# S5 layers of a float32 decoder trunk: order of the stages written by a small list scheduler, float32 in-projections, products moved from GpSimd to VectorE

## Chip, cores and metric

One Trainium2 chip (trn2), one core of it. The metric is device time in microseconds (us) of one execution of the whole program, median of several runs. Engines: TensorE (PE in the profile; PEld is its weight load), VectorE (DVE), ScalarE (ACT), GpSimd (POOL) and SyncE (SP, which here only issues DMAs).

## What is computed

A decoder trunk of four layers on a sequence of T = 512 positions with D = 1024 channels, everything in float32. The layers cycle S5, HGRN2, windowed attention, S5; so layers 0 and 3 are S5. Each layer is `h = h + RMSNorm(branch(RMSNorm(h)))`. The S5 branch, cut to what matters:

```
proj = h @ w_in                       # 1024 x 2048; u = first half, z = second half
xr, xi = einsum(u, bbar_re), einsum(u, bbar_im)   # 64 groups of 16 channels, 64 complex states
s = associative_scan(a, x)            # s[t] = a * s[t-1] + x[t], complex, along the sequence
y = gelu(einsum(c_re, s_re) - einsum(c_im, s_im) + d * u)
y = y * sigmoid(y @ w_glu + b_glu)
out = (y * silu(z)) @ w_out
```

where `a` and `bbar` come from per-group parameters (exp, sin, cos of them).

## The kernel before

**Dense products.** A float32 product of 128 rows of weights with 512 (or 256) columns of activations is made as three products in the float32r type: each operand is split in a high and a low part, and high x high, high x low and low x high are summed (`ws`, `as_`; L146, L160). The weights arrive as raw float32 pieces of 128 x 1024 (`w_load`, tile `wraw`), and `w_conv` splits each: ScalarE copies the high part (`whi`, L112), VectorE subtracts for the low part (`wlo`, L113). The normalised activations are split in the same way by `norm_xt` (`xh` by ScalarE, L210; `xl` by VectorE, L211).

**An S5 layer** (`layer_s5`) works in 16 column blocks of 128 of `w_in`: blocks 0 to 7 give u, 8 to 15 give z. `first_blocks` makes blocks 0 to 3 in two halves of 256 positions each. `s5_tables` computes the small tables of powers of `a` and of rotations from the parameters (`lam`); the sequence is cut in 64 chunks of 8 positions, so that the scan runs over chunks. Then, for each of eight blocks b of 8 groups:

- `s5_block_tables`: loads the block's B and C (`prm`), makes `q`, `vt` (B times powers of a), `w` (C times powers of a), and the taps inside a chunk: `kps`, `kt`, `ktp`, `ksb`, and eight DMAs into `toep`. `vt` is transposed by TensorE (`tps`) into `v`.
- `s5_rot` (once for two blocks): the rotation tables `rot`, copied by DMA into `rotf`.
- `s5_u`: copies the projection to `ut`, writes it to DRAM (`ub`) and reads it back rearranged (`u`).
- `s5_core`: `xps` = v x u on TensorE, swapped halves `xsw` on ScalarE, rotation, real scan and rotation back on VectorE (`xa`, `r`, `rsw`, `spre`), `yps` = u x toep + spre x w on TensorE, gelu into `ysb`, transposes `ytp` into `y`.

Half of the large VectorE products have a partner on GpSimd (`t2`, `t2w`, `rt`, `q12b`, `dmx`, and the subtraction of `w` in odd blocks). After the last block `y` is split into `yh`, `yl` and multiplied with `w_glu` and then `w_out`, as three products each.

**What sets the order.** The text is traced by the Tile framework, which reorders the instructions of each engine by its own cost model and inserts the semaphores. `behind` adds edges that hold some instructions back (`issue_after`). SP issues the weight DMAs, `toep` and `rotf`; ScalarE's queue issues `lam`, `prm`, `dm`, `ub` and `u`. Names in the rows: `pj` is the accumulator of `ws`, `ops` that of the output projection, `t` stands for `t2`, `ap` is the table of powers.

Of the kernel before, what the change touches and what calls it, by code (L numbers as in the profile page):

```python
# [48 lines left out]

class Trunk:  # L50
# [30 lines left out]
    def w_load(self, i):  # L81
        if i >= len(self.wseq) or i in self.wraw or i in self.wcv:
            return
        name, j, c = self.wseq[i]
        shape, pieces = self.w_form(name)
        self.wraw[i] = []
        for v in range(pieces):
            raw = self.wpool.tile(shape, F32, tag="wraw", name="wraw", bufs=3)
            self.nc.sync.dma_start(out=raw, in_=self.a[name][j, c, v])
            self.wraw[i].append(raw)  # L90

    def w_conv(self, i):
        if i >= len(self.wseq) or i in self.wcv:
            return
# [7 lines left out]
        for raw in raws:  # L102
# [72 lines left out]
    def norm_stats(self, L, tbs, h):  # L175

        nc = self.nc
        if tbs[0] == 0:
            self.x = (
                self.act.tile([P, KB, T], F32R, tag="xh", name="xh"),  # L180
                self.act.tile([P, KB, T], F32R, tag="xl", name="xl"),
            )
            self.xs = self.act.tile([P, 4, D], F32, tag="z", name="xs")
# [9 lines left out]
    def norm_xt(self, L, tbs):  # L193
# [7 lines left out]
        for k2 in range(KB // per):  # L201
# [5 lines left out]
            for kk in range(per):  # L207
# [3 lines left out]
                nc.vector.scalar_tensor_tensor(out=xl[:, k, c], in0=ps[:, kk, :], scalar=g, in1=xh[:, k, c].bitcast(F32), op0=ALU.mult, op1=ALU.subtract)  # L211
# [123 lines left out]
    def s5_tables(self, j):  # L335
# [5 lines left out]
        nc.scalar.dma_start(out=lam, in_=a["s5_lam"][j])  # L341
        lr, li, dt = lam[:, 0, :], lam[:, 1, :], lam[:, 2, :]
        nc.scalar.activation(out=dt, in_=dt, func=AF.Exp)
        th = s.tile([P, N], F32, tag="th", name="th", bufs=1)
# [13 lines left out]
        nc.vector.tensor_tensor(out=ap[:, 1, :, 1], in0=mag, in1=sn[:, 0:G], op=ALU.mult)  # L358
        ar, ai = ap[:, 0, :, 1], ap[:, 1, :, 1]
# [64 lines left out]
    def s5_rot(self, pr):  # L424

        nc, s = self.nc, self.scr
        t = self.s5t
        gs = slice(8 * pr, 8 * pr + 8)
        rs = [P, 8, 8, 8]
        rot = s.tile([P, 2, 512], F32, tag="rot", name="rot", bufs=1)  # L430
        rt = self.tab.tile([P, 2, 512], F32, tag="t2", name="rt", bufs=1)
        ro = rot.rearrange("p k (g a b) -> p k g a b", g=8, a=8)
        rr = rt.rearrange("p k (g a b) -> p k g a b", g=8, a=8)
        ea, eb = t["ea"], t["eb"]

        def A(k):
            return bc(ea[:, k, gs, :].unsqueeze(3), rs)

        def Bb(k):
            return bc(eb[:, k, gs, :].unsqueeze(2), rs)  # L440

        nc.vector.tensor_tensor(out=ro[:, 0], in0=A(0), in1=Bb(0), op=ALU.mult)
        nc.gpsimd.tensor_tensor(out=rr[:, 0], in0=A(1), in1=Bb(1), op=ALU.mult)
        nc.vector.tensor_tensor(out=ro[:, 1], in0=A(1), in1=Bb(0), op=ALU.mult)
        nc.gpsimd.tensor_tensor(out=rr[:, 1], in0=A(0), in1=Bb(1), op=ALU.mult)
        nc.vector.tensor_tensor(out=rot[:, 0], in0=rot[:, 0], in1=rt[:, 0], op=ALU.subtract)
        nc.vector.tensor_tensor(out=rot[:, 1], in0=rot[:, 1], in1=rt[:, 1], op=ALU.add)
        out = []
        for i in range(2):
            f = s.tile([P, 2, 512], F32, tag=f"rot{i}", name="rotf", bufs=1)  # L450
# [3 lines left out]
            out.append(f)  # L454
        return out

    def s5_open(self, L):

        self.tabcm = self.tc.tile_pool(name="tab", bufs=1, side="right", reuse_waits="tile")
        self.tab = self.tabcm.__enter__()  # L460
        self.s5_tables(L // 3)

    def s5_block_tables(self, j, b):
        nc, a, s = self.nc, self.a, self.scr
        t = self.s5t
# [12 lines left out]
        s2 = B[:, 3]
        shp = [P, 8, 8, 16]

        vt = self.tab.tile(shp, F32, tag="vt", name="vt", bufs=1)
        t2 = self.tab.tile(shp, F32, tag="t2", name="t2", bufs=1)
        nc.vector.tensor_tensor(out=vt, in0=bc(t["ap"][:, 0, gs, 0:8].unsqueeze(3), shp), in1=bc(q[:, 0].unsqueeze(2), shp), op=ALU.mult)  # L483
# [3 lines left out]
        v = s.tile([P, 8, 128], F32, tag="v", name="v", bufs=2)  # L487
        vtf = vt.rearrange("p g j h -> p g (j h)")
        kps = self.psum.tile([P, 2, 128], F32, tag="ca", name="kps", bufs=2)
        for g in range(8):  # L490
            c = 32 * (g % 4)
            nc.tensor.matmul(kps[c:c + 32, g // 4, :], lhsT=c1[:, g, :], rhs=vtf[:, g, :], start=True, stop=True)
        kt = self.tab.tile([P, 2, 128], F32, tag="q12b", name="kt", bufs=1)
        nc.scalar.activation(out=kt, in_=kps, func=AF.Copy)
        ktp = self.psum.tile([P, 2, 4, 32], F32, tag="ca", name="ktp", bufs=2)
        for i in range(2):
            nc.tensor.transpose(ktp[:, i].rearrange("p g h -> p (g h)"), kt[:, i, :], self.ident)
        dmx = self.tab.tile([P, 8, 16], F32, tag="dmx", name="dmx", bufs=1)
        nc.gpsimd.tensor_tensor(out=dmx, in0=bc(t["dm"][:, gs].unsqueeze(2), [P, 8, 16]), in1=bc(self.cst[:, CO_EYE16:CO_EYE16 + 16].unsqueeze(1), [P, 8, 16]), op=ALU.mult)
        ksb = self.tab.tile([P, 2, 4, 16], F32, tag="ksb", name="ksb", bufs=2)  # L500
        nc.vector.tensor_tensor(out=ksb, in0=ktp[:, :, :, 0:16], in1=dmx.rearrange("p (a g) h -> p a g h", a=2), op=ALU.add)
        toep = self.tp[b % 2]
# [707 lines left out]
```

## Time and profile before

| | |
|---|---|
| median of 3 runs | 1126.23 us (1124.25 to 1127.56) |
| the profiled execution's own time | 1127.56 us |
| its span, first to last instruction | 1125.8 us |
| PE busy | 1039.3 us (92%) |
| DVE busy | 783.4 us (70%) |
| ACT busy | 516.8 us (46%) |
| POOL busy | 233.2 us (21%) |
| granted TensorE clock, mean | 0.968 of 2.4 GHz |

The profile shows one execution. Matmuls are pipelined, and their ends are modelled: an instruction's duration is longer than the distance to the next one, so that a stretch in which PE is "busy" throughout need not be one in which it is at its peak. What one product costs is read from the distance of two starts. In the timeline, "x8" stands for eight like instructions in a row, and the time beside it runs from the first one's start to the last one's end.

### The profile page before, as it was taken

What the parts mean: (1) busy time and instruction counts of PE and PEld (TensorE: products, weight loads), DVE (VectorE), ACT (ScalarE), POOL (GpSimd) and SP (SyncE); (2) the same over time, 40 slices, a digit from 0 to 9 for tenths busy, and PEclk for the clock granted to TensorE, in tenths of its full rate; (3) what the DMA queues carried; (4) which work ended last, traced back from release to release, by engine and by line L of the source; (5) the groups of instructions that cost most, each with busy time, mean ns of one, the idle gap of its engine ahead of it and who ended that gap; (6) DMA issues with size and microseconds to landing.
All of it is one profiled execution on the core that took longest, in us unless ns stands there. A gap on an engine that the chain in (4) does not pass through costs nothing.

```text
span 1125.8 us, 16828 instructions
## 1 busy us (share of the span) xinstructions
PE 1039.3 (92%) x6384; PEld 863.8 (77%) x6384; DVE 783.4 (70%) x1442; ACT 516.8 (46%) x939; POOL 233.2 (21%) x218
## 2 busy tenths in 40 slices
PE   5987898999999999999999989999998888778997
PEld 5866676878899898989888966666688676667885
DVE  6979998675566475656656455566569799995752
ACT  5444444754332324142344344888545254446540
POOL 2165553210200000000001121100011546550200
PEclk9989989999999999999999999999999899998999
DMA  7455425333130212222123443112134644434221
GB/s 244 136 143 141 102 86 128 131 120 114 53 111 22 94 39 83 69 75 76 36 79 102 108 116 100 38 53 80 57 128 126 168 107 139 115 91 140 95 91 56
DMA packets 60320, 112.32 MB, mean 100 GB/s; under 512 B 23632, under 2 KB 33488, under 8 KB 59856
## 3 DMA queue, kind: packets, MB, share of 16 engines
q1 hardware_dynamic: 34272, 87.58, 25.5%
q10 hardware_dynamic: 25968, 23.68, 7.2%
q8 instruction: 50, 0.82, 0.3%
q14 instruction: 30, 0.25, 0.1%
HBM read 87.11 MB, written 8.39 MB: 85 GB/s over the span
## 4 chain that ended last, share of the span: by engine, by line
PE 59%; DVE 23%; issue 6%; DMA 4%; ACT 4%; POOL 3%; ACTq 1%; DVEq 0%; SPq 0%; POOLq 0%
PE pj L146 22%; PE ops L160 14%; PE zps L160 4%; DVE wlo L113 4%; PE vps L160 4%; PE sps L711 2%; PE scps L909 2%; DVE vt L483 2%; PE aops L945 2%; DVE xsw L545 2%; DMA rsw<-rraw 1%; PE ptp L940 1%; DVE vt L485 1%; DMA rotf<-rot 1%; ACT whi L112 1%
## 5 line engine op out<-in xcount | busy, mean ns | idle before, releaser
L146 PE MATMUL pj<-xh,whi 128*128 128x512 f32 (+1 forms) x656 | 238.9, 367 | 0.9 <-ACT whi L112 0.9
L146 PE MATMUL pj<-xh,wlo 128*128 128x512 f32 (+1 forms) x656 | 239.5, 366 | 0.1
L146 PE MATMUL pj<-xl,whi 128*128 128x512 f32 (+1 forms) x656 | 237.9, 364 | 1.3 <-DVE xl L211 1.3
L113 DVE TENSOR_TENSOR wlo<-wraw,whi 128x1024 fp32r<-128x1024 f32 x132 | 172.4, 1311 | 74.5 <-ACT whi L112 67.6
L112 ACT ACTIVATE whi<-wraw 128x1024 fp32r<-128x1024 f32 x132 | 138.6, 1056 | 75.8 <-PE pj L146 31.8
L146 PEld LDWEIGHTS pj<-xh,wlo 128*128 128x128 f32 x656 | 129.0, 197 | 20.6 <-issue 6.1
L146 PEld LDWEIGHTS pj<-xh,whi 128*128 128x128 f32 x656 | 128.9, 198 | 20.5 <-issue 4.8
L146 PEld LDWEIGHTS pj<-xl,whi 128*128 128x128 f32 x656 | 129.0, 197 | 18.2 <-issue 2.7
L160 PE MATMUL ops<-whi,gh 128*128 128x512 f32 x256 | 101.8, 398 | 0.3 <-ACT gh L642 0.3
L160 PE MATMUL ops<-whi,gl 128*128 128x512 f32 x256 | 100.7, 394 | 0.0
L160 PE MATMUL ops<-wlo,gh 128*128 128x512 f32 x256 | 100.3, 392 | 0.0
L160 PEld LDWEIGHTS ops<-whi,gh 128*128 128x128 f32 x256 | 48.2, 188 | 11.3 <-ACT gh L642 1.1
L160 PEld LDWEIGHTS ops<-whi,gl 128*128 128x128 f32 x256 | 48.0, 188 | 11.2 <-DVE gl L643 0.9
L160 PEld LDWEIGHTS ops<-wlo,gh 128*128 128x128 f32 x256 | 48.2, 188 | 10.8 <-issue 1.1
L484 POOL TENSOR_TENSOR t<-ap,q 128x1024 f32<-128x1024 f32 x16 | 40.3, 2519 | 74.6 <-DVE q L475 37.5
L170 POOL TENSOR_SCALAR rs_m<-po_st 128x1 f32<-128x1 f32 x16 | 3.1, 191 | 252.5 <-DVE po_st L256 252.5
L146 PE MATMUL pj<-yh,whi 128*128 128x512 f32 x128 | 49.3, 399 | 4.2 <-ACT yh L621 4.2
L170 POOL TENSOR_SCALAR rs_m<-hss 128x4 f32<-128x4 f32 x8 | 1.6, 194 | 247.9 <-DVE hss L769 247.9
L210 ACT ACTIVATE xh<-xtp,gpre 128x128 fp32r<-128x128 f32 (+1 forms) x96 | 36.2, 400 | 32.8 <-DVE xl L211 20.9
L146 PE MATMUL pj<-yl,whi 128*128 128x512 f32 x128 | 50.1, 393 | 0.0
L146 PE MATMUL pj<-yh,wlo 128*128 128x512 f32 x128 | 50.1, 392 | 0.0
L252 DVE TENSOR_TENSOR yg<-ops,gpost 128x512 f32<-128x512 f32 x32 | 22.0, 689 | 40.0 <-ACT junk L250 39.6
(266 smaller groups left out, 2293.9 us busy)
## 6 DMA issues: line engine op xcount, KB each, us to landing
wraw<-in_s_in SPq DMA_DIRECT2D x32, 512.0 KB, 4.2
wraw<-in_hg_in SPq DMA_DIRECT2D x32, 512.0 KB, 3.5
wraw<-in_at_in SPq DMA_DIRECT2D x20, 512.0 KB, 4.2
rotf<-rot SPq DMA_DIRECT2D x32, 256.0 KB, 4.4
wraw<-in_s_glu SPq DMA_DIRECT2D x16, 512.0 KB, 3.7
wraw<-in_s_out SPq DMA_DIRECT2D x16, 512.0 KB, 3.5
prm<-in_s_bc ACTq DMA_DIRECT2D x16, 256.0 KB, 2.7
ub<-ut ACTq DMA_DIRECT2D x16, 256.0 KB, 3.2
```

Source lines behind the costliest of these rows:

```text
L112: nc.scalar.activation(out=hi, in_=raw, func=AF.Copy)
L113: nc.vector.tensor_tensor(out=lo, in0=raw, in1=hi.bitcast(F32), op=ALU.subtract)
L146: self.nc.tensor.matmul(ps, lhsT=l[k // 4][:, k % 4, c], rhs=r[:, k, n0:n1], start=k == 0 and n == 0, stop=k == KB - 1 and n == 2)
L160: self.nc.tensor.matmul(ps, lhsT=l[:, k, c], rhs=r[k // per][:, k % per, :], start=k == 0 and n == 0, stop=k == KB - 1 and n == 2)
L210: nc.scalar.activation(out=xh[:, k, c], in_=ps[:, kk, :], func=AF.Copy, scale=g)
L252: nc.vector.tensor_tensor(out=yg[:, tb, f], in0=ps, in1=gp[:, f], op=ALU.mult)
L483: nc.vector.tensor_tensor(out=vt, in0=bc(t["ap"][:, 0, gs, 0:8].unsqueeze(3), shp), in1=bc(q[:, 0].unsqueeze(2), shp), op=ALU.mult)
L484: nc.gpsimd.tensor_tensor(out=t2, in0=bc(t["ap"][:, 1, gs, 0:8].unsqueeze(3), shp), in1=bc(q[:, 1].unsqueeze(2), shp), op=ALU.mult)
L545: nc.vector.tensor_tensor(out=xsw, in0=xsw, in1=sin, op=ALU.mult)
L711: nc.tensor.matmul(ps[:, c, :], lhsT=k[:, c * 128:c * 128 + 128], rhs=q4[:, c, :, 1, :], start=True, stop=True)
L909: nc.tensor.matmul(ps[:, bb, lo:256], lhsT=self.q[r, 4 * p + 2 * b2 + bb, qs], rhs=self.k[r, p, ks], start=True, stop=True)
L945: nc.tensor.matmul(ops[64 * i:64 * i + 64].rearrange("p b q -> p (b q)"), lhsT=self.v[:, n - 1 + f, kv * 64:kv * 64 + 64], rhs=pts[i][:, f ...
```

## The change

1. S5's four stages of a block become generators (`s5_v`, `s5_taps`, `s5_w`, `s5_rot`, `s5_u`, `s5_core`), the tables and the 16 in-projections (`s5_rest`) two more. Each yields, ahead of a group of instructions, an engine, a planned duration and the marks that it needs. `Flow.run` takes at each turn the group with the earliest planned start (ties by rank) and lets its generator emit it. The emission runs within `tc.manual_schedule` for PE, DVE, ACT and SP, so that the text's order is the order of these four engines.
2. The in-projections of S5 are made with plain float32 operands, one product in place of three: no split of `w_in` (16 chunks, each 2 pieces, over both layers) and no `xl`. The raw pieces land straight in the tags `whi` and `wlo`, four of each.
3. All products that GpSimd made in the S5 stages are made by VectorE.
4. All DMAs of the S5 stages are issued by SP (`lam`, `prm`, `dm`, `ub`, `u` were ScalarE's).
5. `xps` is made in two column halves of 64 (16 products in place of 8).
6. The order of work within the taps: `v` ahead of `ktp`. The memsets of `s5_tables` move to `s5_open`, for layer 0 ahead of the loads of x. `behind` is no longer used for S5.

```diff
+class Flow:
+    LAG = {"P": 0.25, "V": 0.15, "A": 0.2, "G": 0.2, "D": 4.0}
...
+    def run(self):
+        while self.lines:
+            best = None
+            for e in self.lines:
+                eng, _, needs = e[4]
+                if all(m.t is not None for m in needs):
+                    t = max([self.free[eng], self.seen(e, eng)] + [m.t for m in needs])
+                    if best is None or (t, e[0]) < best[0]:
+                        best = ((t, e[0]), e)
+            (t, _), e = best
+            e[2] = eng = e[4][0]
+            e[1] = self.free[eng] = t + e[4][1]
+            if not self.step(e):
+                self.lines.remove(e)
...
+            if self.plain(i):
+                raw = self.wpool.tile(shape, F32, tag=("whi", "wlo")[v], name="wraw", bufs=4)
...
+        terms = ((hi, xh), (hi, xl), (lo, xh)) if lo is not None else ((hi, xh),)
...
-        nc.scalar.dma_start(out=lam, in_=a["s5_lam"][j])
+        nc.sync.dma_start(out=lam, in_=a["s5_lam"][j])
...
-        nc.gpsimd.tensor_tensor(out=rr[:, 0], in0=A(1), in1=Bb(1), op=ALU.mult)
+        nc.vector.tensor_tensor(out=rr[:, 0], in0=A(1), in1=Bb(1), op=ALU.mult)
...
+        yield "V", 1.3, (m["tables"],) + ((m["kt", b - 1],) if b else ())
...
+        yield "V", 1.2, (m["v", b - 1],) if b else ()
         vt = self.tab.tile(shp, F32, tag="vt", name="vt", bufs=1)
...
+        yield "V", 2.4, ()
-        nc.gpsimd.tensor_tensor(out=t2, in0=bc(t["ap"][:, 1, gs, 0:8].unsqueeze(3), shp), in1=bc(q[:, 1].unsqueeze(2), shp), op=ALU.mult)
+        nc.vector.tensor_tensor(out=t2, in0=bc(t["ap"][:, 1, gs, 0:8].unsqueeze(3), shp), in1=bc(q[:, 1].unsqueeze(2), shp), op=ALU.mult)
...
+        yield "P", 0.7, (m["vt", b],)
...
+        yield "D", 0.6, (m["y", b - 2],) if b > 1 else ()
+        d["toep"] = toep = self.tp[b % 2]
         for jj in range(8):
...
+        yield "D", 0.2, ()
         ub = self.dram.tile([8, 128, 64], F32, tag="ub", name="ub", bufs=8)
-        nc.scalar.dma_start(out=ub.rearrange("j f c -> f j c"), in_=ut)
+        nc.sync.dma_start(out=ub.rearrange("j f c -> f j c"), in_=ut)
...
+        yield "P", 1.3, (m["v", b], m["u", b], m["rot", b]) + ((m["xa", b - 1],) if b else ())
         for g in range(8):
-            nc.tensor.matmul(xps[:, g, :], lhsT=t["v"][:, g, :], rhs=u[:, g, :], start=True, stop=True)
+            for o in (0, 64):
+                nc.tensor.matmul(xps[o:o + 64, g, :], lhsT=d["v"][:, g, o:o + 64], rhs=u[:, g, :], start=True, stop=True)
...
+                for _ in self.ws_steps(ps[b][:, c], w[b // 2], b % 2, self.x, c.start, c.stop):
+                    yield "P", 0.43, ()
...
+                yield "P", 0.0, (m["ev", n - 4],)
+                ps_ = self.pj()
+                for _ in self.ws_steps(ps_, w, fb, self.x, 0, T):
+                    yield "P", 0.86, ()
...
+        with self.scratch("left"), self.tc.manual_schedule(engines={E.PE, E.DVE, E.Activation, E.SP}):
...
+            flow.add(tables(), 0)
             for b in range(8):
+                flow.add(self.s5_core(b, m), 10 * b + 1)
+                flow.add(self.s5_v(j, b, m), 10 * b + 2)
+                flow.add(self.s5_taps(b, m), 10 * b + 3)
+                if b % 2 == 0:
+                    flow.add(self.s5_rot(b // 2, m), 10 * b + 4)
+                flow.add(self.s5_w(b, m), 10 * b + 5)
+                flow.add(self.s5_u(b, ps, m), 10 * b)
+            flow.add(self.s5_rest(L, ps, m), 100, 0.0 if L else 12.0)
+            flow.run()
```

The planned durations of the tables are 4, 4, 3, 2 and 3 us. Where the list gives a group `"V"` and 2.4 us, it holds two VectorE products of 1.2 us.

## Rows read from the trace of the kernel before

**Rows 1.** Stretches: us; busy PE, PEld, DVE, ACT, POOL; clock; DMA share, GB/s.
```profile
13.00:203.00 190.00, 163.58 (x1140) 134.54 (x1141) 177.52 (x260) 94.81 (x159) 78.88 (x58) 0.94 0.46 124
203.00:290.00 87.00, 86.73 (x389) 71.13 (x388) 54.04 (x63) 44.23 (x71) 15.57 (x18) 1.00 0.38 127
839.00:1033.00 194.00, 163.21 (x1133) 134.02 (x1132) 171.44 (x254) 91.03 (x152) 80.12 (x62) 0.91 0.43 119
```

**Rows 2.** The chain that ended last, where glu becomes dense: start, us, what.
```profile
202.95 10.71 PE pj L146 x47
...
1033.15 41.05 PE pj L146 x181
```

**Rows 3.** Timeline of PE, in-projections: first one, then dense halves and wholes.
```profile
13.46 0.58 PE L146 MATMUL pj<-xh,whi 128*128 128x256 f32 x1 [0.87 <-ACT whi L112]
...
843.04 0.28 PE L146 MATMUL pj<-xl,whi 128*128 128x256 f32 x1
...
844.00 0.28 PE L146 MATMUL pj<-xh,whi 128*128 128x256 f32 x1
...
184.17 0.40 PE L146 MATMUL pj<-xh,whi 128*128 128x512 f32 x1
...
187.15 0.39 PE L146 MATMUL pj<-xl,whi 128*128 128x512 f32 x1
```

**Rows 4.** Plain float32 products: one run in the timeline, and all by form.
```profile
330.33 1.46 PE L698 MATMUL dps<-hq,hk 128*128 128x192 f32 x8
...
L698 PE MATMUL dps<-hq,hk 128*128 128x192 f32 x64 | 12.9, 334 | 0.7 <-DVE st L701 0.7
```

**Rows 5.** Timeline of PE, one block's small products between in-projections.
```profile
86.51 0.64 PE L492 MATMUL kps<-vt,c 128*32 128x128 f32 x16 [1.40 <-DVE vt L485]
87.09 0.49 PE L146 MATMUL pj<-xh,wlo 128*128 128x512 f32 x1
...
88.00 0.39 PE L568 MATMUL yps<-w,spre 128*64 128x128 f32 x4
88.22 0.39 PE L566 MATMUL yps<-toep,u 128*64 128x128 f32 x4
...
92.41 0.39 PE L146 MATMUL pj<-xh,whi 128*128 128x512 f32 x1
92.82 0.44 PE L566 MATMUL yps<-toep,u 128*64 128x128 f32 x4
93.19 0.50 PE L146 MATMUL pj<-xl,whi 128*128 128x512 f32 x1
```

**Rows 6.** VectorE groups of the S5 blocks, whole run: busy us, mean ns | idle before.
```profile
L483 DVE TENSOR_TENSOR vt<-ap,q 128x1024 f32<-128x1024 f32 x16 | 40.4, 2525 | 0.2
L514 DVE TENSOR_TENSOR w<-ap,c 128x1024 f32<-128x1024 f32 x16 | 19.4, 1213 | 0.0
L545 DVE TENSOR_TENSOR xsw<-xsw,rotf 128x512 f32<-128x512 f32 x16 | 26.2, 1636 | 0.0
L553 DVE TENSOR_TENSOR rsw<-rsw,rotf 128x512 f32<-128x512 f32 x16 | 10.9, 679 | 0.0
L548 DVE TENSOR_TENSOR_SCAN r<-mdec,xa 128x512 f32<-128x512 f32 x16 | 21.6, 1347 | 0.2
```

**Rows 7.** Layer 0's tables: timeline marks, and what else VectorE did from 21.9 to 52.3.
```profile
16.95 0.28 ACT L343 ACTIVATE lam<-lam 128x96 f32<-128x96 f32 x1
...
21.93 0.24 DVE L346 TENSOR_TENSOR th<-lam 128x96 f32<-128x96 f32 x1
...
51.69 0.69 DVE L442 TENSOR_TENSOR rot<-ea,eb 128x512 f32<-128x512 f32 x1
...
L113 DVE TENSOR_TENSOR wlo<-wraw,whi 128x1024 fp32r<-128x1024 f32 x5 | 6.1, 1225 | 0.0
L211 DVE SCALAR_TENSOR_TENSOR xl<-xtp,gpre,xh 128x128 fp32r<-128x128 f32 (+1 forms) x18 | 6.2, 362 | 0.5 <-ACT xh L210 0.5
```

**Rows 8.** Timeline of SP's queue: one group of `toep` DMAs.
```profile
61.45 5.29 SPq L505 DMA_DIRECT2D toep<-ksb  x8
```

More of the change, by code (lines that the diff above doesn't have):

```diff
@@ L1 @@
 import math
+from collections import defaultdict
 from contextlib import ExitStack, contextmanager
@@ L47, with __init__, add, seen @@
 ATSEQ = "c00 q2 c01 q3 c02 c03 z0 c10 z1 c11 g00 g01 z2 g02 g03 c12 z3 c13 g10 g11 g12 g13".split()
+class Mark:
+    def __init__(self):
+        self.t = None
+class Flow:
+    LAG = {"P": 0.25, "V": 0.15, "A": 0.2, "G": 0.2, "D": 4.0}
+    def __init__(self):
+        self.free = dict.fromkeys(self.LAG, 0.0)
+        self.lines = []
+    def add(self, line, rank, t=0.0):
+        e = [rank, t, None, line, None]
+        if self.step(e):
+            self.lines.append(e)
+    def seen(self, e, eng):
+        return e[1] + (0 if e[2] is None or (e[2] == eng and eng != "D") else self.LAG[e[2]])
+    def step(self, e):
+        while True:
+            r = next(e[3], None)
+            if r is None:
+                return False
+            if isinstance(r, Mark):
+                r.t = self.seen(e, None)
+            else:
+                e[4] = r
+                return True
+    def run(self):
[12 more added lines that the diff above has]
+                self.lines.remove(e)
 class Trunk:
@@ L491, in s5_block_tables @@
             c = 32 * (g % 4)
-            nc.tensor.matmul(kps[c:c + 32, g // 4, :], lhsT=c1[:, g, :], rhs=vtf[:, g, :], start=True, stop=True)
+            nc.tensor.matmul(kps[c:c + 32, g // 4, :], lhsT=d["c1"][:, g, :], rhs=vtf[:, g, :], start=True, stop=True)
+        yield "A", 0.4, ()
         kt = self.tab.tile([P, 2, 128], F32, tag="q12b", name="kt", bufs=1)
         nc.scalar.activation(out=kt, in_=kps, func=AF.Copy)
+        v = self.scr.tile([P, 8, 128], F32, tag="v", name="v", bufs=2)
+        for hh in range(2):
+            yield "P", 0.45, (m["states", b - 2],) if b > 1 else ()
+            tps = self.psum.tile([P, 4, 128], F32, tag="ca", name="tps", bufs=2)
+            for g in range(4):
+                nc.tensor.transpose(tps[:, g, :], vtf[:, 4 * hh + g, :], self.ident)
+            yield "A", 0.6, ()
+            nc.scalar.activation(out=v[:, 4 * hh:4 * hh + 4, :], in_=tps, func=AF.Copy)
+        d["v"] = v
+        yield m["v", b]
+        yield "P", 0.25, ()
         ktp = self.psum.tile([P, 2, 4, 32], F32, tag="ca", name="ktp", bufs=2)
@@ L514, in s5_block_tables @@
[L514 to L519 removed]
+        yield m["toep", b]
@@ L583, in s5_core, with s5_rest @@
                     in_=ytp, func=AF.Copy)
+    def s5_rest(self, L, ps, m):
+        nc = self.nc
+        w = [self.w_next("s5_in"), self.w_next("s5_in")]
+        for b in range(4):
+            ps[b] = self.pj()
+        for half in range(2):
+            c = slice(half * 256, half * 256 + 256)
+            for b in range(4):
+                if half == 0 and b == 3:
+                    for _ in self.norm_xt(L, (2,)):
+                        pass
+                for _ in self.ws_steps(ps[b][:, c], w[b // 2], b % 2, self.x, c.start, c.stop):
+                    yield "P", 0.43, ()
+                if half:
+                    yield m["ps", b]
+            if half == 0:
+                for _ in self.norm_xt(L, (3,)):
+                    pass
+        for c in range(6):
+            w = self.w_next("s5_in")
+            for fb in range(2):
+                n = 4 + 2 * c + fb
+                yield "P", 0.0, (m["ev", n - 4],)
+                ps_ = self.pj()
+                for _ in self.ws_steps(ps_, w, fb, self.x, 0, T):
+                    yield "P", 0.86, ()
+                if c < 2:
+                    ps[n] = ps_
+                    yield m["ps", n]
+                else:
+                    yield "A", 0.6, ()
+                    nc.scalar.activation(out=self.z[:, 2 * (c - 2) + fb, :], in_=ps_, func=AF.Copy)
+                    yield m["ev", n]
     def layer_s5(self, L):
```

221 lines of the change are left out of this document (130 added, 91 removed).

## Prediction

> **What bounds the kernel now.** I read the stretches first, because the change touches only the S5 layers, and ask in each which engine has no slack [rows 1]. In the glu stage PE is busy for 86.7 of 87 us at full clock: nothing that frees another engine can shorten it. In the two S5 stretches it is otherwise. PE is busy for 163.6 of 190 us and 163.2 of 194 us, at a granted clock of 0.94 and 0.91, that is, part of the time at 1.2 GHz; VectorE is busy for 177.5 and 171.4 us. So both are nearly full by the busy rows, and busy rows of PE overstate its work. I therefore count PE's work from distances of starts.
>
> A float32r product of 256 columns starts 0.12 us after the one before it (8 steps from 843.04 to 844.00), one of 512 columns 0.229 us (13 steps from 184.17 to 187.15) [rows 3]. The in-projections of an S5 layer are 192 of the former (4 blocks x 2 halves x 8 x 3) and 288 of the latter (12 x 8 x 3): 23.0 + 66.0 = 89.0 us. The rest of PE's work per block: `kps` 0.58; `yps` 32 instructions at 4 per 0.22 us, 1.76; 14 transposes of 128 columns at 0.108 (by the pace per column below), 1.51; `xps`, priced by `yps`, 1.76: 5.6 us, 44.9 for eight blocks [rows 4, 5]. Entering and leaving a burst of 64-column tiles costs 0.41 - 0.229 = 0.18 and 0.37 - 0.22 = 0.15 us [rows 5]; with one such burst per block, 2.6. The second half's 16 transposes of x add 1.7. Sum: 138.2 us per layer.
>
> The stage has more time than that. Its first product is at 13.5 in layer 0, at 839 in layer 3 [rows 1, 3]. Its end I take from the chain: glu becomes dense at 202.95 and at 1033.15, where 181 of glu's 192 products (8 blocks x 8 x 3) still lie ahead, so 11 x 0.229 = 2.5 us were made before [rows 2]. The effective ends are 200.4 and 1030.6. PE thus loses 200.4 - 13.5 - 138.2 = 48.7 us in layer 0 and 53.4 in layer 3, to waits and to the lower clock. These 102 us are what a better order can win. What holds PE is mostly VectorE: product `vt` takes 2.525 us where `w`, of the same shape, takes 1.213, and `xsw` 1.636 where `rsw` takes 0.679 [rows 6]; the slow ones have a GpSimd product beside them in the text.
>
> **The change part by part.**
>
> *Float32 in-projections.* In the trace a plain float32 product is two instructions (`dps`: 32 products in the text, 64 in the row), and in a run of eight they start (1.46 - 0.33) / 7 = 0.161 us apart for 192 columns, 0.84 ns per column [rows 4]. So 256 columns cost 2 x 0.215 = 0.43 us, 512 cost 0.861, against 0.36 and 0.687 for three float32r ones. Per layer 64 x 0.43 + 96 x 0.861 = 110.3 us, 21.3 more than before. The bounds are narrow: the row is of the same form, and only a lower clock would raise it.
>
> *No splits.* In layer 0 the splits of weights and x cost VectorE 1.2 and 0.36 us each [rows 7]; 16 of the first and 24 of the second per layer make some 28 us. ScalarE loses its part too. Both come off engines that PE waits for, so they are worth only what PE's loss shrinks.
>
> *Products to VectorE.* Per block VectorE then has 6 products of 128x1024 at 1.213, 7.3; five small ones at about 0.5 (at most 0.68), 2.5; half of 6 rotation products at 0.68, 2.0; the core's six at 0.68 and a scan at 1.35, 5.4 [rows 6]: 17.2 us, 138 per layer, with no GpSimd product beside them. If the clean prices did not hold, `vt`'s 2.5 us is the other bound: 8 x 2 x 1.3 = 21 us more, still below PE's time.
>
> *Tables.* In layer 0 they take VectorE from 21.93 to 51.69, 29.8 us; 12.3 of these are `wlo` and `xl`, and `w`, `q` take some 1.5 more: 16 us of their own [rows 7]. VectorE's total is 154 us per layer, PE's is more: PE becomes the bound.
>
> *`xps` in halves.* 32 instructions of 64 columns in two column tiles. Nearest are `yps` (4 per 0.22: 1.76 us) and `kps` (16 in 0.58: 1.2 us); without overlap of the halves it would be 3.5. I take 1.76, no change. A second tiled burst per block costs another 0.33 x 8 = 2.6 us [rows 5]. The Trainium skill, TensorEngine Tiling (Array Packing), section Key Properties, says that a change of tiling mode drains TensorE; by that rule every alternation of in-projections and tiled bursts has to pay, as the two tolls show.
>
> PE's work after: 110.3 + 44.9 + 5.3 + 1.7 = 162.2 us per layer.
>
> *The order.* The list gives PE an in-projection step whenever nothing of a block is ready, so PE should be without idle time except where the emitted order waits for something late. Three such waits I price. (a) Cold start in layer 0: the first half product takes 0.58 us, the dense ones 0.28 [rows 3], so PE begins at half clock; 3 us (0 to 6). (b) Late tables. The text puts `kps` of block 0 after 22.6 us of its plan (tables 16, then `q`, `vt`), with in-projections from 12 on: 24 half steps. On the chip PE is there at 13.5 + 3 + 24 x 0.43 = 26.8. The tables need `lam`, which now sits on SP's queue behind x and the first weights; ScalarE's exp of it ran at 16.95 before [rows 7]. From 16: 16 + 16 + 5.6 = 37.6, 11 us late, and everything behind on PE waits; I take 8, since `lam` may be read sooner (0 to 12). In layer 3 the plan starts both at 0: PE is there at 839 + 22.4, `vt` at 839 + 5 + 21.6 if VectorE starts 5 us behind: 3 us (0 to 6). (c) Scatter: planned durations that miss by some per cent; 4 us per layer (1 to 25, half of the present loss). Then 1.2 us until glu starts: a copy and a product of y, about 0.6 each by the nearest row of that shape.
>
> *DMAs to SP.* Eight `toep` DMAs hold SP for 5.29 us [rows 8] where the plan counts 0.6. Their successors on the queue are `rotf`, `u`, `ub` and weights. I cost it at nothing: `toep` of block b can go out a whole block (20 us) ahead of its use, `u` has three buffers. Without that cover see the second rival.
>
> *Sum.* Layer 0: 162.2 + 3 + 8 + 4 + 1.2 = 178.4 us, end at 191.9, gain 8.5. Layer 3: 162.2 + 3 + 4 + 1.2 = 170.4, end at 1009.4, gain 21.2. VectorE would end at 16 + 154 + 6 = 176 and 844 + 154 + 6 = 1004, earlier in both. The profiled execution's 1127.6 less 29.7 is 1097.9; it lies 1.3 above the median of the runs, so 1097.
>
> **The rivals.**
>
> *The order fits without waits.* Only the cold start and the y step remain: ends at 179.9 and 1002.4, gain 48.7, 1078 us. For it: PE always has an in-projection to run. Against: `lam` behind 3 MB of loads. With the tolls gone and `xps` at 1.2 it would be 1060.
>
> *SP's queue becomes the bound; slower.* Everything is on one queue, and a `toep` group that the plan counts as 0.6 us takes 5.29. If a block's `u` or `rotf` stands behind it and its core waits for half a group, PE, in the text's order, waits 2.65 us per block: 16 x 2.65 = 42.4, 1097 + 42 = 1139. It decides from 29.7 / 16 = 1.9 us per block. For it: `rotf` did stand directly behind `toep` in the old order. Against: the slack of a block. The Trainium skill, DMA: Bandwidth & Descriptors, section Issuing engines are not separate DMA queues, says that spreading DMAs over issuing engines saves only sequencer issue time; by that rule the move costs just that, and the row says that this is 0.65 us a piece here.
>
> *A wash.* The fixed order leaves PE 15 us more of scatter per layer (19 in all, still under half of the 49 to 53 now): the gain is gone, about 1127. This is also what is left if the order of the four engines is not the text's, and Tile's own order remains with 42.6 us more of PE work and less of VectorE's.
>
> **How the numbers follow.** My forecast has 0.52 (its own range 1082 to 1115, from the bounds of (b) and (c)), the fit without waits 0.23, the wash 0.1, the slower case 0.15. The measurement can tell about 0.3% (3.4 us) from no change. Faster by more: 0.77; within it: 0.08; slower: 0.15. Below 1066 I leave out a tenth (tolls and `xps` at their lower bounds), above 1132 another.
>
> **What the profile after would show.** In both S5 stretches PE's clock near 1.0 and PE dense; `pj` in two instructions of 0.43 us; `vt` and `xsw` at 1.21 and 0.68 us; VectorE less busy than 171 us; one wait of PE for `vt` near 27 us of 8 us or so. I am wrong if PE's waits in the stretches for `u`, `rotf`, `toep` add up to over 15 us a layer, if VectorE stays full, or if the first block comes without any wait.

## The result, and the profile after

The changed kernel takes 1117.98 us (median of 5 runs) where the kernel before takes 1124.69: ratio 0.993, 95% interval 0.991 to 0.9949. Run again (e0_after below) it took 1117.18, ratio 0.9918, 0.9891 to 0.9946. So it is faster, by 0.7 to 0.8%, some 9 us; 29.7 were forecast. One of the five executions, the profiled one, ran with the clock lowered over its whole length (0.844) and is left out of the ratio; all rows of the changed kernel here are of e0_after, whose span is 1116.7 us against 1125.8 before.

I compare layers by one stretch: from the first in-projection product to the first product of the output projection, which stands behind glu. First the busy rows of the two layers in the kernel before, then in the changed one (start:end, length, busy PE, PEld, DVE, ACT, POOL, PE's clock, DMA share, GB/s):

```profile
13.46:243.86 230.40, 204.44 (x1321) 168.33 (x1321) 204.20 (x289) 116.50 (x190) 90.36 (x58) 0.95 0.45 127
838.96:1074.05 235.09, 204.29 (x1314) 168.04 (x1313) 198.84 (x283) 113.52 (x185) 92.05 (x70) 0.93 0.42 121
```
```profile
13.90:247.26 233.36, 210.79 (x1290) 137.88 (x1289) 177.62 (x292) 100.04 (x174) 11.59 (x8) 0.95 0.43 125
840.52:1063.36 222.84, 207.83 (x1282) 136.78 (x1280) 181.19 (x295) 99.14 (x170) 15.58 (x25) 0.96 0.46 130
```

Layer 3 became 12.3 us shorter, layer 0 became 3.0 us longer. The prediction's gains of 8.5 and 21.2 us would have ended layer 0 at 235.4 and made layer 3 213.9 us long (both with the start of the kernel before). PE's idle time (length less busy) went from 26.0 to 22.6 us in layer 0 and from 30.8 to 15.0 in layer 3. VectorE lost its overload as forecast: 177.6 of 233 us, and 181.2 of 223.

Where PE stands idle its timeline shows, in the changed kernel: the first products, the in-projections' pace, the two waits before the first `kps`, and the ends of both layers; below it, the clock around the waits and near the ends.

```profile
13.90 1.22 PE L222 MATMUL pj<-xf,wraw 128*128 128x256 f32 x2
14.91 1.22 PE L286 MATMUL xtp<-cst,xs 128*128 128x128 f32 x8
15.97 10.09 PE L222 MATMUL pj<-xf,wraw 128*128 128x256 f32 x46
25.90 1.04 PE L286 MATMUL xtp<-cst,xs 128*128 128x128 f32 x8
26.78 1.03 PE L222 MATMUL pj<-xf,wraw 128*128 128x256 f32 x4
43.16 1.08 PE L593 MATMUL kps<-vt,c 128*32 128x128 f32 x16 [15.35 <-DVE vt L579]
44.17 2.08 PE L222 MATMUL pj<-xf,wraw 128*128 128x256 f32 x4
...
112.73 1.88 PE L222 MATMUL pj<-xf,wraw 128*128 128x512 f32 x4
114.45 0.60 PE L602 MATMUL tps<-cst,vt 128*128 128x128 f32 x4
...
247.26 0.39 PE L237 MATMUL ops<-whi,gh 128*128 128x512 f32 x1
...
873.54 1.08 PE L593 MATMUL kps<-vt,c 128*32 128x128 f32 x16 [7.51 <-DVE vt L579]
...
1063.36 0.39 PE L237 MATMUL ops<-whi,gh 128*128 128x512 f32 x1
```
```profile
13.00:28.00 15.00, 14.81 (x73) 12.52 (x71) 11.01 (x53) 7.76 (x21) 0.44 (x1) 1.00 0.63 236
28.00:43.00 15.00, 0.00 (x0) 0.00 (x0) 14.42 (x43) 0.71 (x3) 0.00 (x0) 0.65 0.00 0
43.00:50.00 7.00, 6.84 (x35) 5.40 (x36) 6.21 (x9) 0.98 (x2) 0.00 (x0) 0.54 0.47 107
50.00:180.00 130.00, 126.60 (x851) 73.21 (x849) 101.44 (x139) 56.61 (x98) 0.00 (x0) 1.00 0.51 135
180.00:210.00 30.00, 26.18 (x173) 16.46 (x173) 18.29 (x24) 12.63 (x20) 0.00 (x0) 0.89 0.23 77
...
874.00:880.00 6.00, 6.00 (x31) 4.74 (x24) 5.63 (x8) 0.99 (x3) 0.00 (x0) 0.60 0.47 99
...
985.00:1010.00 25.00, 19.00 (x123) 11.06 (x121) 18.19 (x24) 12.35 (x20) 0.00 (x0) 0.86 0.44 133
```

Two things are to be seen. The pace is what the prediction took: 46 instructions from 15.97 to 25.90 are 0.216 us each (a product is two: 0.43), and 4 from 112.73 to 114.45 are 0.43 (0.86). And the late tables cost twice: 15.35 us of waiting, and behind it PE at half clock (0.54 is near the lower level of 1.2 GHz), where four instructions take 2.08 us that took 1.03 before. The chain now shows dense glu from 210.23 and 1032.17 on, but these can't be set beside the 202.95 and 1033.15 of [rows 2]: by the timeline 28 and 54 of glu's 192 products are made before them, where it was 11. By the first product of the output projection, glu's end is 3.4 us later in layer 0 (247.26 for 243.86) and 10.7 us earlier in layer 3 (1063.36 for 1074.05).

VectorE's groups answer to [rows 6]: `vt` and `xsw`, slow before, have the clean price.

```profile
L575 DVE TENSOR_TENSOR vt<-ap,q 128x1024 f32<-128x1024 f32 x16 | 19.4, 1214 | 0.0
L680 DVE TENSOR_TENSOR xsw<-xsw,rotf 128x512 f32<-128x512 f32 x16 | 10.9, 682 | 0.0
...
L616 DVE TENSOR_TENSOR ksb<-ktp,dmx 128x128 f32<-128x128 f32 x16 | 4.7, 291 | 41.7 <-PE ktp L610 41.5
```

The last row shows that VectorE now stands 41.5 us in front of `ksb`, waiting for PE (9.8 us in the kernel before). The tables of layer 0 answer to [rows 7]: SP's queue, where `lam` stands behind x and the first weights, and VectorE's first and last steps up to `vt`.

```profile
0.72 4.94 SPq L1261 DMA_DIRECT2D x<-in_x  x4
5.70 1.17 SPq L152 DMA_DIRECT2D wraw<-in_s_in  x2
6.92 0.43 SPq L422 DMA_DIRECT2D lam<-in_s_lam  x1
```
```profile
15.14 0.26 DVE L428 TENSOR_TENSOR th<-lam 128x96 f32<-128x96 f32 x1 [0.92 <-ACT lam L424]
...
19.34 0.28 DVE L439 TENSOR_TENSOR ap<-mag,cos 128x64 f32<-128x64 f32 x1 [1.78 <-ACT cos L413]
...
37.06 0.42 DVE L564 TENSOR_TENSOR q<-prm,co 128x256 f32<-128x256 f32 x1
...
41.79 1.22 DVE L579 TENSOR_TENSOR vt<-vt,t 128x1024 f32<-128x1024 f32 x1
```

The tables take 37.06 - 15.14 = 21.9 us, with no other work of VectorE between them and one wait of 1.78 us for ScalarE, where the prediction took 16. In layer 3 they run from 845.64 to 867.45, 21.8 us, with one step of the normalisation between them.

### The profile page after: what moved, and what is told of

The parts are those of the page before. It is cut to its first block, busy times and chain, and to the rows that moved or that the text cites. A ratio compares the mean times of both kernels' runs of the same rounds, so it can differ in the third digit from the quotient of the medians.

```text
span 1184.9 us, 16469 instructions
## 1 busy us (share of the span) xinstructions
PE 1140.3 (96%) x6320; PEld 834.7 (70%) x6320; DVE 735.9 (62%) x1450; ACT 483.9 (41%) x907; POOL 79.7 (7%) x130
## 4 chain that ended last, share of the span: by engine, by line
PE 86%; DVE 9%; ACT 2%; issue 1%; POOL 1%; DMA 1%; ACTq 0%; DVEq 0%; POOLq 0%; SPq 0%
PE pj L222 41%; PE ops L237 14%; PE vps L237 5%; PE zps L237 4%; PE sps L891 3%; PE scps L1089 3%; PE aops L1125 2%; PE xps L669 2%; PE yps L706 1%; PE tps L602 1%; PE yps L708 1%; PE ptp L1120 1%; PE dps L878 1%; DVE pw L396 1%; DVE wlo L183 1%
## 5 line engine op out<-in xcount | busy, mean ns | idle before, releaser
L222 PE MATMUL pj<-xf,wraw 128*128 128x512 f32 (+1 forms) x640 | 273.5, 580 | 0.0
L222 PEld LDWEIGHTS pj<-xf,wraw 128*128 128x128 f32 x640 | 123.0, 201 | 96.9 <-issue 83.7
L183 DVE TENSOR_TENSOR wlo<-wraw,whi 128x1024 fp32r<-128x1024 f32 x100 | 125.4, 1262 | 82.2 <-ACT whi L182 75.5
L222 PE MATMUL pj<-xh,whi 128*128 128x512 f32 (+1 forms) x336 | 126.1, 376 | 0.0
L222 PE MATMUL pj<-xh,wlo 128*128 128x512 f32 (+1 forms) x336 | 125.2, 373 | 0.0
L222 PE MATMUL pj<-xl,whi 128*128 128x512 f32 (+1 forms) x336 | 124.6, 371 | 0.0
L222 PEld LDWEIGHTS pj<-xh,whi 128*128 128x128 f32 x336 | 65.4, 195 | 14.3 <-issue 3.6
L222 PEld LDWEIGHTS pj<-xh,wlo 128*128 128x128 f32 x336 | 65.5, 195 | 12.8 <-issue 2.0
L222 PEld LDWEIGHTS pj<-xl,whi 128*128 128x128 f32 x336 | 65.4, 195 | 11.7 <-issue 1.2
L237 PEld LDWEIGHTS ops<-wlo,gh 128*128 128x128 f32 x256 | 49.3, 193 | 15.4 <-issue 1.4
L237 PE MATMUL vps<-wlo,xh 128*128 128x256 f32 x160 | 46.7, 292 | 0.0
```

What stands on the lines that cost most here:

```text
L237: self.nc.tensor.matmul(ps, lhsT=l[:, k, c], rhs=r[k // per][:, k % per, :], start=k == 0 and n == 0, stop=k == KB - 1 and n == 2)
```

## The experiments

The unchanged changed kernel, for the profile above:

> The changed kernel once more, for a profile at the clock at which its times were taken. Theory A (PE is dense except while the tables are late): one wait of PE for vt in layer 0 of 12 to 15 us, all other waits of PE in the two stretches under 10 us together, in-projection products of 512 columns in 0.86 us, clock near 1.0; glu dense at 195 to 199 and at about 1024. Rival B (the fixed order makes PE wait for u, rotf or toep): such waits add up to over 15 us in a layer. Rival C (float32 products cost more than the prediction took): products of 512 columns take over 0.90 us at full clock. Time 1117 to 1119.

1117.18 us. Theory A held for layer 0's wait (15.35, a little over its 12 to 15) and the pace; PE's waits for `toep` and `u` are 1.7 and 0.9 us in all, so B and C fell. PE's other idle time in the two layers is 22.6 + 15.0 - 15.35 = 22.2 us, not under 10. Counted back from glu's end as in [rows 2] (181 products, 40.9 us), glu is dense at 206.4 in layer 0, 7 us or more later than A said, and at 1022.5 in layer 3, about as A said: in layer 0 more than the one wait is lost.

**The late tables of layer 0.** e1_start0 lets the in-projections begin at the plan's 0.

```
-            flow.add(self.s5_rest(L, ps, m), 100, 0.0 if L else 12.0)
+            flow.add(self.s5_rest(L, ps, m), 100, 0.0)
```


> The plan of layer 0 lets the in-projections begin at 0 like layer 3, not at 12. Theory A: 28 more steps of 0.43 us stand ahead of kps of block 0, so PE's wait for vt falls from 13 to about 1 to 3 us and those steps are missing later, where PE is dense: 9 to 12 us less, about 1107. Rival (VectorE's chain, which begins with the tables, sets the end of the stretch, and PE's wait is only where it shows): the wait of 13 us goes, but later waits of the same sum take its place, time within 3 us of 1118.

1104.23 us, ratio 0.981 (0.9777 to 0.9843): 13 us better than the changed kernel, theory A and a little more than its 9 to 12. The layer row and the first block:

```profile
13.69:230.99 217.30, 208.00 (x1290) 137.13 (x1290) 177.06 (x291) 99.89 (x173) 11.73 (x8) 0.98 0.46 133
```
```profile
43.42 0.64 PE L593 MATMUL kps<-vt,c 128*32 128x128 f32 x16 [1.52 <-DVE vt L579]
44.00 0.70 PE L222 MATMUL pj<-xf,wraw 128*128 128x256 f32 x2
```

The same `vt` is there at the same time; only PE has 14 us more work ahead of it. Idle time falls by 13.3 us, the layer by 16.1; PE's busy time falls by 2.8 as well, and `kps`, 1.08 us long before, takes 0.64: the lower clock is gone. e9_lam_act brings the tables forward instead, e7_dma_act moves the other DMAs too.

```
e9:  lam            nc.sync.dma_start -> nc.scalar.dma_start
e7:  lam, s5_d, prm, ub, u            -> nc.scalar.dma_start
```


> The changed kernel with the DMA of lam alone on ScalarE's queue; prm, s5_d, ub and u stay on SP's. Theory (e7's 7 us are all the earlier lam in layer 0): 1108 to 1112, first kps at 38 to 39. Rival (they come from u and ub off SP's queue): 1115 to 1119.

> The changed kernel with the DMAs of lam, s5_d, prm, ub and u back on ScalarE's queue, at the same places of the text. Theory (SP's queue is no bound): within 4 us of 1117; lam comes some 2 us sooner in layer 0, so up to 3 us less. Rival of the prediction (SP's queue holds the blocks): the waits for u and toep go and it is 5 to 15 us faster.

e9: 1112.59 us (0.9868, 0.9842 to 0.9894). e7: 1110.15 (0.9849, 0.9827 to 0.9871). With `lam` on the other queue the first `kps` comes at 38.64, after a wait of 9.89 us:

```profile
38.64 1.08 PE L593 MATMUL kps<-vt,c 128*32 128x128 f32 x16 [9.89 <-DVE vt L579]
```

So 4.6 of e7's 7.0 us are `lam`, which a place in a queue had cost; e9's theory held for `kps` and missed its time by 0.6 us. e7's time lies in the range of its rival, not of its theory, but for the most part not for the rival's reason: the changed kernel's waits for `toep` and `u` were 2.6 us in all, and e7 has 1.7. The other 2.4 us lie inside the two intervals; e9's waits for `toep` and `u` are 2.4 us longer than e7's (4.1 for 1.7). For most of the gain SP's queue was not the bound.

**The same cure in layer 3.** e5_tables_plan plans the tables at 23 and 27 us; e10_plan_l3 moves layer 3 alone, and less, to 22.

```
e5:  yield "V", 4.0 / 4.0 / 3.0 / 2.0 / 3.0
  -> yield "V", (10.0 if j else 6.0) / 6.0 / 4.5 / 2.5 / 4.0,  in-projections from 0.0
e10: the first group alone: 10.0 if j else 4.0,                 in-projections from 0.0
```


> As e1_start0, and the tables planned at the lengths that the trace shows (23 us in layer 0; 26.5 in layer 3, where VectorE starts late), not 16. Theory (a plan with the true lengths lets PE run on until vt is there): the waits of 7.5 us in layer 3 and 1.5 in layer 0 go, and some low clock behind them: 8 to 10 us under e1_start0, 1094 to 1097. Rival (in-projections spent early are missing late: PE waits in the last blocks for VectorE instead): within 3 us of 1104.

> As e1_start0, and in layer 3 alone the first group of the tables planned at 10 us, not 4, so that PE comes to kps about 6 us later, still before vt. Theory (e5 overshot: in it PE came to kps after vt was ready, and ran out of in-projections early): PE's wait for kps in layer 3 falls from 7.5 to 1 or 2 us without new waits, 1097 to 1100. Rival (in layer 3 in-projections spent early are missing late, whatever the overshoot): within 3 us of 1104.

1107.43 (0.9825, 0.9799 to 0.9851) and 1107.05 us (0.9825, 0.98 to 0.9851): in both the theory fell, 3 us worse than e1_start0. In e5 PE has no wait before the first `kps` of either layer, yet both layers are no shorter (220.4 and 224.0 us for e1's 217.3 and 223.6): later waits came in their place, for `toep` (8.9 us in all, 1.7 in e1), `yh` and `vt`, as the rival said, though only in part for VectorE. In e10 layer 3's wait for the first `vt` is 0.6 us in place of 7.5, yet the layer is longer, 226.9 us:

```profile
828.09:1054.94 226.85, 211.02 (x1282) 138.96 (x1280) 181.17 (x296) 98.19 (x170) 15.20 (x25) 0.95 0.45 127
```
```profile
PE yps L706 <- DMA toep<-ksb: 11.0, 4, 4.3
```
```profile
973.95 5.00 SPq L621 DMA_DIRECT2D toep<-ksb  x8
```
```profile
980.75 0.70 PE L706 MATMUL yps<-toep,u 128*64 128x128 f32 x4 [4.30 <-DMA toep<-ksb]
981.20 0.67 PE L708 MATMUL yps<-w,spre 128*64 128x128 f32 x4
```

PE now waits 11.0 us for `toep` (1.7 in the changed kernel), 2.9, 4.3 and 2.8 of them in layer 3. The eight DMAs hold SP from 973.95 for 5.00 us, and PE reaches `yps` before they land: the plan counts 0.6 for the group. (The next group of `yps` starts 0.45 us later, not 0.22: half clock again.) e12_toep_plan gives the group its length; e15_toep_two issues half of it elsewhere.

```
e12: yield "D", 0.6 -> yield "D", 5.0          (toep, on top of e10)
e15: (nc.scalar if jj % 2 else nc.sync).dma_start(out=toep[...   (on top of e10)
```


> As e10_plan_l3, and a group of toep DMAs planned at 5.0 us, as it holds SP's queue, not 0.6. Theory (the waits of yps for toep in layer 3, 2.9, 4.3 and 2.8 us, come from a plan that thinks toep is there 4 us before it is): they fall under 1.5 us each, 1098 to 1103. Rival (nothing in the text can hide it, since the block's own chain is late): the waits move to other tiles, 1104 to 1110.

> As e10_plan_l3, with every second toep DMA issued on ScalarE's queue, so that a group is out in some 2.5 us. Theory (the time of issue, 5.0 us on SP's queue, makes toep late): the waits for toep in layer 3 shrink by 2 us each, 1099 to 1104. Rival (ScalarE loses as much, four times 0.6 us per block in the way of evacuations): 1106 or more.

1103.15 us (0.9784, 0.9763 to 0.9805) and 1102.86 (0.9781, 0.9761 to 0.9801). Both theories held in the main: PE's waits for `toep` fall from 11.0 to 3.1 and 4.1 us, and layer 3 takes 220.1 and 221.2 us, now less than the changed kernel's 222.8. One wait of 3.1 us stays in e12, so its "under 1.5 each" did not hold. And both edits reach layer 0 too, which became longer: 220.6 us in e12 and 219.8 in e15, 217.8 in e10, with a wait of 4.0 and 4.6 us for one `vt` in place of 2.0.

**The parts by themselves.** In the kernel before: e2_before_f32 has only the float32 in-projections, e3_before_dve only GpSimd's products on VectorE.

```
e2: -  for n, (l, r) in enumerate(((hi, xh), (hi, xl), (lo, xh))):
    +  terms = ((hi, xh), (hi, xl), (lo, xh)) if lo is not None else ((hi, xh),)
e3: nc.gpsimd.tensor_tensor -> nc.vector.tensor_tensor   (rr, q2, t2, dmx, w)
```


> The kernel before with the float32 in-projections alone (no xl, no split of their weights), products on GpSimd and the old order as they are. By the prediction's terms PE has 21.3 us more per layer, VectorE some 28 us less. Theory (before, PE waits for VectorE, so the splits are worth more than the products cost): 1105 to 1120. Rival (PE's work decides): 1150 to 1168, twice 13 to 21 us more.

> The kernel before with the products of the S5 blocks on VectorE alone in place of GpSimd, float32r in-projections and the old order as they are. VectorE gets some 4.5 us of products more per block (36 per layer); vt falls from 2.5 to 1.2 us and xsw from 1.6 to 0.68, some 19 us per layer. Theory (VectorE was full and is now fuller by 17 us a layer): 1140 to 1160. Rival (the slow products, not their number, held PE): 1105 to 1120.

e2: 1159.61 us (1.0292, 1.0254 to 1.0329), the rival. The prediction's 21.3 us a layer are real cost: of the 42.6 us 33.4 are seen, so that the splits that go can have given back only some 9. e3: 1124.81 (0.999, 0.9968 to 1.0012), neither case: `vt` fell to 1.217 us, and the time did not move. In the changed kernel the two parts were taken back one at a time:

```
e6: nc.vector.tensor_tensor -> nc.gpsimd.tensor_tensor   (rr, q2, t2 twice, dmx)
e4: plain() returns False; x is the pair (xh, xl); steps planned at 0.36 and 0.69;
    each split adds its VectorE time to the plan
```


> The changed kernel with six products per block (two of rot every second block, q12b, t2 twice, dmx) back on GpSimd, which is not in the planned order. Theory (beside a GpSimd product VectorE is slow: vt 2.5, xsw 1.6 us, and each GpSimd product is a longer step in the way to kps): 8 to 30 us slower than 1117. Rival (VectorE has slack now, where its products run makes no difference): within 4 us of 1117.

> The changed kernel with the three float32r products, xl and the weight splits back in its in-projections, planned at 0.36 and 0.69 us a step, with the order otherwise planned as it is. Theory (the 0.161 us row was right, and PE is the bound of the changed kernel, so float32 costs it what e2 showed, 33 us, less what VectorE's splits take): 1085 to 1105. Rival (with the splits VectorE has 182 us a layer and becomes the bound): 1118 to 1140.

e6: 1137.2 us (1.0082, 1.006 to 1.0104), the theory's range: what cost nothing in the old order costs 20 us in this fixed one, whose plan was not told of GpSimd. VectorE stands in front of `w` for GpSimd's product, and `xsw` and `rsw` take longer (0.68 us each in the changed kernel); `vt` stayed at 1.21 us, not the theory's 2.5:

```profile
L637 DVE TENSOR_TENSOR w<-w,t2w 128x1024 f32<-128x1024 f32 x16 | 19.6, 1225 | 20.6 <-POOL t2w L635 20.1
L680 DVE TENSOR_TENSOR xsw<-xsw,rotf 128x512 f32<-128x512 f32 x16 | 17.8, 1115 | 0.0
L691 DVE TENSOR_TENSOR rsw<-rsw,rotf 128x512 f32<-128x512 f32 x16 | 23.9, 1495 | 0.0
```

e4: 1186.7 us (1.0521, 1.0488 to 1.0555), worse than either case. PE's waits, the three largest:

```profile
PE yps L703 <- DMA toep<-ksb: 41.5, 9, 14.7
PE kps L590 <- DVE xl L289: 20.3, 1, 20.3
PE xtp L283 <- DVE xl L289: 12.9, 4, 6.8
```

The splits stand in VectorE's fixed order, and blocks behind them are late. How much of the 69 us a better place for them would win was not tried, so this does not price float32r; it shows that less PE work did not help in this order. The last part, e8_xps_whole:

```
-            for o in (0, 64):
-                nc.tensor.matmul(xps[o:o + 64, g, :], lhsT=d["v"][:, g, o:o + 64], ...
+            nc.tensor.matmul(xps[:, g, :], lhsT=d["v"][:, g, :], ...
```


> The changed kernel with xps in eight products of 128 columns, as before, not sixteen halves. Theory (the halves run side by side: 32 instructions in 1.09 us by the fast trace, against 1.70 for the 16 of before): 16 x 0.6 = 10 us slower, 1124 to 1130. Rival (the prediction's price, 1.76 us either way): within 3 us of 1117.

1127.07 us (0.9999, 0.9989 to 1.0009): 10 us slower than the changed kernel, as the theory said. First the changed kernel, then e8: 32 instructions in 1.08 us, 16 in 1.73.

```profile
95.38 1.15 PE L669 MATMUL xps<-u,v 128*64 128x64 f32 x32
96.46 1.13 PE L222 MATMUL pj<-xf,wraw 128*128 128x512 f32 x2
```
```profile
96.34 1.89 PE L668 MATMUL xps<-u,v 128*128 128x64 f32 x16
98.07 5.37 PE L222 MATMUL pj<-xf,wraw 128*128 128x512 f32 x12
```

**Added up.** e11_both has `lam` on ScalarE's queue, layer 0's in-projections from 4.0 and e10's layer 3; e13_l0_only has layer 3 as in the changed kernel; e14_l0_act adds e7's other DMAs; e16_all adds e12's two plan lengths, in layer 3 alone.

```
e13: lam on nc.scalar;  100, 0.0 if L else 4.0
e11: e13 + first table group 10.0 if j else 4.0
e14: e13 + s5_d, prm, ub, u on nc.scalar
e16: e14 + first table group 10.0 and toep 5.0, in layer 3
```


> lam on ScalarE's queue, in-projections of layer 0 planned from 4 (so PE comes to kps at about 36, vt is there at 38.5), and e10's layer 3. Theory (waits and tables add up): layer 0 ends about 5 us before that of e1_start0: 1093 to 1099. Rival (the end of the blocks' chain or PE's work sets layer 0 already): 1102 to 1106.

> e11_both with layer 3 planned as in the changed kernel. Theory (e10's layer 3 costs 3 us against the plan as it was, and the two layers do not touch each other): 1094 to 1097. Rival (it made no difference): 1098 to 1100.

> e13_l0_only with s5_d, prm, ub and u on ScalarE's queue too. Theory (e7 against e9 was 2.4 us, and it stays): 1 to 3 us under e13_l0_only. Rival (e7's surplus was another place in the order of layer 0, which is not there in this plan): within 1.5 us of it.

> e14_l0_act, and in layer 3 the first group of the tables planned at 10 us and a toep group at 5.0 us, as in e12_toep_plan. Theory (the layers add up; e12's layer 3 took 220.1 us from its first in-projection to its first output product, e14's 222.7): 2 to 3 us under e14_l0_act, 1090 to 1092. Rival (with u and ub on ScalarE's queue SP is free enough, and the plan of toep gives nothing more): 1093 to 1095.

e11 1098.9 us (0.9752, 0.9723 to 0.9781), e13 1096.71 (0.9734, 0.9718 to 0.9751), e14 1093.89 (0.9713, 0.9686 to 0.9741), e16 1091.81 (0.9681, 0.965 to 0.9712). All four lie in the ranges of their theories, but single steps of 2 to 3 us lie within the intervals; the way from 1117 to 1092 does not. The layers of e16:

```profile
14.28:222.25 207.97, 203.91 (x1289) 134.11 (x1289) 176.21 (x282) 97.64 (x168) 11.96 (x8) 1.00 0.49 138
817.13:1037.11 219.98, 206.54 (x1281) 136.27 (x1280) 181.19 (x296) 99.39 (x170) 15.24 (x25) 0.98 0.46 127
```

Layer 0 has 4.1 us of idle time left, at a clock of 1.00. Layer 3 still has 13.4; the largest waits are 3.4 us for `yh`, 3.1 for one `toep`, and 1.9 and 1.4 for `vt`.

## Why the prediction was off

The direction was right, the size was not: 1097 against 1117.2 to 1118.0. The wide range held it, the likeliest case's own range (to 1115) did not. In stretches: layer 0 should have taken 235.4 - 13.5 = 221.9 us and took 233.4, layer 3 213.9 and took 222.8; together 20.4 us too long, which is the miss.

**The step that failed is (b), the late tables.** It was put at 8 us in layer 0 (0 to 12) and 3 in layer 3 (0 to 6), and measured 15.35 and 7.51, over both bounds. The cause was right: PE stood before `kps` for the tables. The place, PE arriving at 27.8 for 26.8, was right in part by luck: the 3 us of (a) were not there, but 16 transposes of x and two more half products were. The tables' length was wrong. I had taken `wlo`, `xl` and `w`, `q` out of the 29.8 us of [rows 7] as if the work were laid end to end. Left alone the same small steps take 21.9 us, not 16. The rows show why. Two steps of `m`, of which the second needs the first, start 0.25 us apart in the changed kernel; in the kernel before a step of another chain of the tables (`red_n`) starts between them, 0.14 us after the first:

```profile
23.05 0.22 DVE L468 TENSOR_TENSOR m<-mag 128x64 f32<-128x64 f32 x1
23.30 0.23 DVE L469 TENSOR_TENSOR m<-m 128x64 f32<-128x64 f32 x1
```
```profile
26.61 0.22 DVE L385 TENSOR_TENSOR m<-mag 128x64 f32<-128x64 f32 x1
26.75 0.25 DVE L331 TENSOR_TENSOR red_n<-red_n,th 128x96 f32<-128x96 f32 x1
26.92 0.22 DVE L386 TENSOR_TENSOR m<-m 128x64 f32<-128x64 f32 x1
```

So steps that wait for one another leave gaps. In them the splits and the tables' own other chains had run, and the order fixed in the text puts each chain by itself. Of the 5.9 us, 1.8 are the wait for ScalarE; that the gaps make up the rest is argued, the length is measured. The rest of layer 0's miss is a discount: the prediction's own sum put `vt` 11 us late and took 8, since `lam` might be read sooner, but VectorE began only 0.9 us sooner (15.14 for 16).

e1_start0 shows what that one term is worth in layer 0: 16.1 us of the layer, more than the wait itself, since no sum of mine had a clock that drops behind a long wait. That is 7 x 0.46 = 3.2 us in layer 0 and 6 x 0.40 = 2.4 in layer 3 by the clock rows.

**Other terms.** (a), the cold start, was 3 us and came to some 0.6: the first two in-projection instructions take 1.01 us (13.90 to 14.91), where two take 0.43 later. The clock row reads 1.00 there all the same, so at this place it does not tell the pace. `xps` in halves was priced at 1.76 us either way and is 1.08 against 1.73, about 10 us over both layers in the prediction's favour (e8). The in-projections were right to a hundredth (0.216 and 0.43 us an instruction). So PE's work was 162.2 - 8 x 0.68 = 156.8 us a layer, and the scatter that I took as 4 + 1.2 us was 22.57 - 15.35 = 7.2 and 15.01 - 7.51 = 7.5 us of idle time, with another 30 x 0.11 = 3.3 us of lower clock near the end of layer 0 and 25 x 0.14 = 3.5 near that of layer 3. With glu's 43.5 us (192 products and what lies between, as before) layer 0 sums to 156.8 + 15.4 + 3.2 + 7.2 + 3.3 + 43.5 = 229.4, 4.0 short of 233.4, and layer 3 to 156.8 + 7.5 + 2.4 + 7.5 + 3.5 + 43.5 = 221.2, 1.6 short of 222.8. In layer 0 most of that is PE's work priced too low: e16, where the clock is 1.00 there, shows PE busy for 203.9 us, 3.6 more than 156.8 + 43.5. From start to start `yps` takes 15.9 us a layer there, where the prediction took 14.1, and the transposes 16.0 for 13.8.

The miss of 20.4 us is then (b) with 7.4 + 4.5, the lower clock behind its waits with 5.6, scatter with 2.0 + 2.3, the lower clock near the ends with 6.8 and work with 5.6, less 10.9 for `xps` and some 3 for (a). That it was not half as large again is luck: `xps` hid it.

**What held.** VectorE came down to a load below PE's, at clean prices: 151.4 us busy from 13 to 210, where the prediction took 154. PE's clock did not come near 1.0 over the stretches: it is 0.95 and 0.96, for the waits of (b) and the ends. PE's waits for `u`, `rotf` and `toep` stayed under 15 us a layer, so the slower rival fell in this order. It was not empty: `toep`'s 5 us on the queue, counted as 0.6, became PE's largest wait in the two layers (11.0 us) under another plan (e10), and fell to 3.1 when the plan knew of it (e12) and 4.1 when the queue was shared (e15). The Trainium skill, DMA: Bandwidth & Descriptors, section Issuing engines are not separate DMA queues, says that spreading the issue saves only sequencer time; e15 agrees, since that time is what was late.

**Where the gain went.** Alone in the old order float32 costs 33 us (e2) and the moved products nothing (e3); the changed kernel is 9 us better than before, so if these add, the order with the halves (10 us) is worth some 42 us, and most of that pays for float32. That they add is not shown: the moved products are worth nothing in the old order and 20 us in the new one (e6), and the new order was not run with the old products and a plan made for them. The order has 25 us more to give with five lengths and places in it put right (e16, 1091.8 for 1117.2). Why layer 3, with its first wait gone, keeps 13.4 us of idle time, most of it in its second half, is not settled; moving its tables ahead of the layer was not tried.

## What to carry to other kernels

An order fixed in the text can't step around a late operand. Each planned length that was wrong (tables 16 for 21.9 us, a DMA group 0.6 for 5.0) could become a wait of TensorE at that very place. A true length is no cure by itself: with the tables' own lengths in the plan (e5) the first waits went, others came, and the time was 3 us worse than with the in-projections merely begun earlier (e1_start0). Small dependent steps must be measured alone; time taken out of a mixed stretch is not additive. And filling one wait may only bring the next one up: e10 removed 7 us of waiting in layer 3 and gained nothing until the DMA behind it was planned too.

## What the runs showed of the hardware

A float32 product over two column tiles of 64 runs its halves side by side, at least in part: 32 instructions in 1.08 us against 16 full ones in 1.73. One after another, at the in-projections' pace of 0.43 us for 512 columns, 32 instructions of 64 columns would take 1.72. The Trainium skill, TensorEngine Tiling (Array Packing), section Key Properties, says that different tiles work in parallel; this trace agrees.

After 15 us without a product TensorE's granted clock was 0.54 in the next 7 us; after 7.5 us without one it was 0.60 in the next 6 us. Such a wait cost itself and 2.4 to 3.2 us more. The Trainium skill, TensorE: Matmul & The Clock Gate, section Part 1: The HAM clock gate, says that an idle engine falls back to 1.2 GHz; the trace agrees.
